# No GpSimd weight parts beside the first half of the gates' table, and every fourth expert tile there in plain float32

## Chip, cores and metric

One core of a Trainium2 chip runs the kernel. The metric is the device time of one execution in microseconds (us); smaller is better. TensorE (PE) multiplies, VectorE (DVE), ScalarE (ACT) and GpSimd (POOL) work on elements, SyncE (SP) issues most of the transfers.

## What is computed

A transformer layer, then two more. The first layer ends in a feed-forward part called PEER: each of its 256 tokens picks 128 of 16,384 single-neuron experts by product keys. The changed code lies in that part alone:

```python
q = (ht @ w_q).reshape(T, PEER_HEADS, PEER_QDIM)
s1 = einsum('thd,nd->thn', q[..., :PEER_HALF], sub_k1)
s2 = einsum('thd,nd->thn', q[..., PEER_HALF:], sub_k2)
...
gates = jax.nn.softmax(vals, axis=-1)
...
```

For the chosen experts, with input rows `expert_u` and output rows `expert_v`, the output is the sum over experts of gate times gelu(h · u) times v. Everything is float32.

## The kernel before

The kernel doesn't gather experts. It computes all 16,384 of them for all tokens and multiplies by a table of gates that is zero where an expert wasn't chosen. The experts come in 64 blocks of 256, and each block has two tiles (j = 0, 1) of 128 experts. `peer_block` (L983) does this in stages:

- **Heads** (L1044 to L1076): scores and top-16 lists. A queue of side work (`Side`) is stepped between them. It holds the keys' side products of later layers, and then `expert_in` of blocks 0 to 15 (`AHEAD`, L985).
- **Index work** (L1081 to L1145): VectorE turns the lists into the gates' coordinates. The side queue is stepped here too.
- **First half of the table**, `build_gates(0)` (L1203): 32 steps of 8 tokens. In each, VectorE makes one-hot tiles `o2` (L1169) and `o1` (L1171) and two scaled copies `og` (L1175), PE multiplies them in 16 small matmuls (L1178), and ACT copies the result into the table `G` (L1181). Between the steps the side queue advances by 21 tiles in all (`left`, L1202): tile 1 of block 5, and blocks 6 to 15.
- **Outgoing blocks 0 to 15** (L1207): `expert_out` scales the activations by the gates and multiplies them with `v` into four PSUM accumulators.
- **Blocks 16 to 63** (L1214): `expert_in(b + 1)`, with steps of `build_gates(1)` between while there are any, then `expert_out(b)`.

A float32 product is made in one of two ways. The **split** way (`wsplit`, `split_into`, `mm3`): ACT rounds the weights to `whi` (L295), another engine subtracts to get `wlo` (L296), and three matmuls in a reduced float32 format add up to full precision (L309 to L311), 24 for one expert tile with its eight slices of the model's width. The **plain** way (L1007): PE multiplies the raw weights `wraw` and the float32 activations `h2F`, eight matmuls for a tile, with no work on ACT or VectorE. `native[0]` chooses: it is False in the heads, True in the index work (set at L1079), and False again from L1148. Who subtracts is set by `K.pool_every`: with 2 (L1147) every second weight tile goes to GpSimd, with 0 all go to VectorE; L1206 sets 0 after the first half of the table.

Weights arrive by SP in transfers of 1 MB, a block's `u` or `v`, into three `wraw` buffers taken in turn. In blocks 16 to 63 the order is u(b+1), v(b), u(b+2), v(b+1), so the transfer of v(b+1) takes the buffer of u(b+1) and waits for its last reader. The split parts have three buffers each. Each engine runs its instructions in the order in which a planner put them.

`h2F` (8 KB in a partition) lies in the pool `p2f`, which closes with the index work. The pool `p2a` (16 activations of 2 KB) closes at L1209, and `p2h` (one table quarter of 32 KB) opens in its place.

Of the kernel before, what the change touches and what calls it, by code (L numbers as in the profile page):

```python
# [9 lines left out]
F32 = mybir.dt.float32  # L10
# [10 lines left out]
S = 256  # L21
NT = 2
KD = D // 128
# [941 lines left out]
def mem_values(K, pool2, mT, layer, tag):  # L965

    nc = K.nc
    for n in range(2):
        ps = [K.ps(tag) for _ in range(NT)]
        yield from K.gemm_tok_gen(ps, mT, f"xv{layer}", n * 4, 8)  # L970
        for t in range(NT):
            o = K.t(pool2, [128, 512], F32, tag="kvo")
            nc.scalar.activation(o, ps[t], AF.Copy)
            nc.sync.dma_start(K.kv[layer][:, t * D + n * 512:t * D + (n + 1) * 512], o)
# [8 lines left out]
def peer_block(K, x1, mT, close_mem):  # L983
# [5 lines left out]
    with ExitStack() as ctx:  # L989
        P = K.pool("p2", 1, ctx, side="right")  # L990
        P2 = K.pool("p2b", 2, ctx, side="right")
        ahead = ExitStack()
# [1 line left out]
        h2T = K.new_xT()  # L994
        GA = {}

        native = [False]

        def expert_in(b, tag="f"):
            ps = K.ps(tag)  # L1000
            pv = ps.rearrange("p (j n) -> p j n", j=2)
            raw = K.raw(("u", b), K.ins["u"][b].rearrange("p j k e -> p j (k e)"))
            for j in range(2):
                if native[0]:

                    for k in range(KD):
                        nc.tensor.matmul(pv[:, j], raw[:, j, k * 128:(k + 1) * 128], h2F[:, k, :],  # L1007
                                         start=k == 0, stop=k == KD - 1)
                else:
                    K.gemm_feat(pv[:, j], h2T, K.wsplit(raw[:, j], 8))  # L1010
                if j == 0:
                    yield
            GA[b] = K.t(GAP, [128, 2, S], F32, tag="ga") if b < AHEAD else K.t(P2, [128, 2, S], F32, tag="ga2")
            nc.scalar.activation(GA[b], pv, AF.Gelu_apprx_tanh)
            yield

        with ExitStack() as c2:
            F = K.pool("p2f", 1, c2)
            h2F = K.t(F, [128, KD, S], F32, tag="h2F")
            with ExitStack() as c3:  # L1020
                K.tmp = K.pool("tmp2", 2, c3)
                K.rms_T(K.tmp, x1, "norm2", h2T, h2F)
# [9 lines left out]
            def top16(src, val, idx, scr):  # L1032
# [5 lines left out]

            side = Side(mem_values(K, K.mt, mT, 0, "acc"), mem_values(K, K.mt, mT, 1, "acc"),
                        *[expert_in(b, "acc") for b in range(AHEAD)])  # L1040
            side.step(RS)
            K.pool_every = 1
# [33 lines left out]
                side.step(KVH)  # L1076
            pending.pop()()
            K.pool_every = 0
            native[0] = True  # L1079

            io16 = K.t(R, [128, 16], BF16, tag="io16")  # L1081
            nc.vector.tensor_copy(io16, K.cst("iota16"))
# [61 lines left out]
                nc.vector.tensor_copy(GP[:, 0, sl], GT[:, sl])  # L1144
                nc.vector.tensor_tensor(GP[:, 1, sl], GT[:, sl], GP[:, 0, sl], op=ALU.subtract)  # L1145

            K.pool_every = 2  # L1147
            native[0] = False  # L1148

        close_mem()  # L1150
        PG = K.pool("p2g", 2, ctx)
# [3 lines left out]
        def build_gates(half):  # L1155
            for q in (2 * half, 2 * half + 1):
                G[q] = K.t(PG2 if q == 2 else PG, [128, 32, S], F32, tag="G")
            b2, b1 = [128, 4, 128, 2], [128, 4, 64, 2]
            io2 = iota2[:, None].to_broadcast(b2)
            io1 = iota2[:, None, half * 64:half * 64 + 64].to_broadcast(b1)  # L1160

            def tokens(a, t0, shape):
                return a[:, t0:t0 + 8].rearrange("p (a b) -> p a b", a=4)[:, :, None, :].to_broadcast(shape)

            for t0 in range(0, S, 8):
                ps = K.ps()
                pv = ps.rearrange("p (t n) -> p t n", t=8)
                o2 = K.t(P2, b2, F16, tag="o2", bufs=GBUF)
                nc.vector.tensor_tensor(o2, io2, tokens(IT[1], t0, b2), op=ALU.is_equal)  # L1169
                o1 = K.t(P2, b1, F16, tag="o1", bufs=GBUF)  # L1170
                nc.vector.tensor_tensor(o1, io1, tokens(IT[0], t0, b1), op=ALU.is_equal)  # L1171
                og = []
                for j in range(2):
                    og.append(K.t(P2, b1, F16, tag=f"og{j}", bufs=GBUF))
                    nc.vector.tensor_tensor(og[j], o1, tokens(GP[:, j], t0, b1), op=ALU.mult)  # L1175
                for i in range(8):
                    for j in range(2):
                        nc.tensor.matmul(pv[:, i], o2[:, i // 2, :, i % 2], og[j][:, i // 2, :, i % 2],  # L1178
                                         start=j == 0, stop=j == 1, skip_group_check=True)
                for q in range(2):  # L1180
                    nc.scalar.activation(G[2 * half + q][:, :, t0:t0 + 8],  # L1181
                                         pv[:, :, q * 32:(q + 1) * 32].rearrange("p t n -> p n t"), AF.Copy)
                yield
# [27 lines left out]
        side = Side(build_gates(1))  # L1211
        for _ in expert_in(AHEAD):
            pass
        for b in range(AHEAD, 64):  # L1214
            if b < 63:
                for _ in expert_in(b + 1):
                    side.step(1)
            expert_out(b)
# [243 lines left out]
def layer_kernel(ctx: ExitStack, tc: tile.TileContext, ins, out):  # L1462
# [34 lines left out]
    K.mt = K.pool("mt", 2, held)  # L1497
    x1, mem = attention_block(K, x)
    x2 = peer_block(K, x1, mem, held.close)
    K.tmp = K.pool("tmp3", 2)  # L1500
    xT = K.new_xT()
# [29 lines left out]
```

## Time and profile before

| | us |
|---|---|
| median of 3 runs (1878.97 to 1880.27) | 1879.25 |
| the profiled execution | 1878.24 |
| its span in the trace | 1876.4 |
| PE busy | 1827.8 (97%) |
| VectorE busy | 1230.8 (66%) |
| ACT busy | 924.5 (49%) |
| GpSimd busy | 242.7 (13%) |

The span is from the first to the last instruction on the core; some 2 us around it belong to the execution's own time. Busy times of engines overlap. A matmul's duration holds its way through the array, so the time that it costs is read from the starts of matmuls that follow each other, not from the durations. An engine that is not the bound may idle at no cost.

### The profile page before, as it was taken

What the parts mean: (1) busy time and instruction counts of PE and PEld (TensorE: products, weight loads), DVE (VectorE), ACT (ScalarE), POOL (GpSimd) and SP (SyncE); (2) the same over time, 40 slices, a digit from 0 to 9 for tenths busy, and PEclk for the clock granted to TensorE, in tenths of its full rate; (3) what the DMA queues carried; (4) which work ended last, traced back from release to release, by engine and by line L of the source; (5) the groups of instructions that cost most, each with busy time, mean ns of one, the idle gap of its engine ahead of it and who ended that gap; (6) DMA issues with size and microseconds to landing.
All of it is one profiled execution on the core that took longest, in us unless ns stands there. A gap on an engine that the chain in (4) does not pass through costs nothing.

```text
span 1876.4 us, 31063 instructions
## 1 busy us (share of the span) xinstructions
PE 1827.8 (97%) x12627; PEld 1648.9 (88%) x12627; DVE 1230.8 (66%) x2094; ACT 924.5 (49%) x1527; POOL 242.7 (13%) x149
## 2 busy tenths in 40 slices
PE   7999999999999999999999999999999999989998
PEld 5798989889788989999999998988999899979997
DVE  5757657999866777555555557555566766646667
ACT  5554458445554555444444445443555545425453
POOL 2710237033000000000000000111100111120000
PEclk9999999999999999999999999999999999989999
DMA  7541445443454444555555557553556556525552
GB/s 268 180 158 46 136 171 191 161 177 114 159 197 173 168 164 174 177 183 180 188 193 181 182 191 284 180 178 114 177 183 201 183 180 204 199 90 202 173 190 110
DMA packets 78320, 326.39 MB, mean 174 GB/s; under 512 B 5856, under 2 KB 6496, under 8 KB 69600
## 3 DMA queue, kind: packets, MB, share of 16 engines
q1 hardware_dynamic: 74864, 315.35, 48.8%
q10 hardware_dynamic: 3312, 9.05, 1.4%
q8 instruction: 99, 1.62, 0.3%
q14 instruction: 45, 0.37, 0.1%
HBM read 321.23 MB, written 3.15 MB: 173 GB/s over the span
## 4 chain that ended last, share of the span: by engine, by line
PE 90%; DVE 6%; ACT 1%; DMA 1%; POOL 1%; issue 1%; ACTq 0%; POOLq 0%; SPq 0%; DVEq 0%
PE f L309 14%; PE f L311 14%; PE f L310 14%; PE acc L310 12%; PE acc L309 12%; PE acc L311 12%; PE acc L1007 2%; PE t L1178 1%; DVE og L1175 1%; PE acc L793 1%; DMA wraw<-in_stream 1%; PE f L1386 1%; PE acc L769 1%; DVE wlo L296 1%; PE t L395 1%
## 5 line engine op out<-in xcount | busy, mean ns | idle before, releaser
L295 ACT ACTIVATE whi<-wraw 128x1024 fp32r<-128x1024 f32 x528 | 557.3, 1057 | 575.9 <-PE f L310 311.5
L296 DVE TENSOR_TENSOR wlo<-wraw,whi 128x1024 fp32r<-128x1024 f32 x463 | 570.1, 1232 | 376.5 <-ACT whi L295 375.8
L309 PE MATMUL f<-xTh,whi 128*128 128x256 f32 x2016 | 574.1, 285 | 2.5 <-ACT xTh L295 2.5
L311 PE MATMUL f<-xTh,wlo 128*128 128x256 f32 x2016 | 573.6, 285 | 0.0
L310 PE MATMUL f<-xTl,whi 128*128 128x256 f32 x2016 | 572.5, 284 | 0.5 <-DVE xTl L296 0.5
L309 PEld LDWEIGHTS f<-xTh,whi 128*128 128x128 f32 x2016 | 386.5, 192 | 10.4 <-ACT xTh L295 3.4
L310 PEld LDWEIGHTS f<-xTl,whi 128*128 128x128 f32 x2016 | 387.0, 192 | 6.2 <-DVE xTl L296 1.2
L311 PEld LDWEIGHTS f<-xTh,wlo 128*128 128x128 f32 x2016 | 387.1, 192 | 2.5 <-issue 0.7
L296 POOL TENSOR_TENSOR wlo<-wraw,whi 128x1024 fp32r<-128x1024 f32 x65 | 160.0, 2470 | 556.3 <-ACT whi L295 390.3
L310 PE MATMUL acc<-wlo,wth 128*128 128x512 f32 x512 | 190.9, 396 | 0.0
L311 PE MATMUL acc<-whi,wtl 128*128 128x512 f32 x512 | 186.3, 395 | 1.1 <-DVE wtl L296 1.1
L309 PE MATMUL acc<-whi,wth 128*128 128x512 f32 x512 | 175.8, 397 | 0.9 <-ACT wth L295 0.9
L311 PEld LDWEIGHTS acc<-whi,wtl 128*128 128x128 f32 x512 | 96.0, 188 | 24.3 <-DVE wtl L296 1.5
L309 PEld LDWEIGHTS acc<-whi,wth 128*128 128x128 f32 x512 | 96.3, 188 | 22.5 <-ACT wth L295 1.0
L310 PEld LDWEIGHTS acc<-wlo,wth 128*128 128x128 f32 x512 | 96.2, 188 | 21.0
L295 ACT ACTIVATE wth<-gw 128x256 fp32r<-128x256 f32 x128 | 52.4, 411 | 83.7 <-PE acc L310 80.7
L1239 POOL MEMSET sgw<- 64x256 f32 x1 | 0.3, 307 | 671.6 <-DVE wlo L296 671.6
L1175 DVE TENSOR_TENSOR og<-o,gp 128x512 f16<-128x512 f16 x128 | 69.7, 554 | 23.3 <-PE t L1178 23.3
L296 DVE TENSOR_TENSOR wtl<-gw,wth 128x256 fp32r<-128x256 f32 x128 | 53.9, 423 | 34.3 <-ACT wth L295 19.2
L310 PE MATMUL acc<-wlo,xTh 128*128 128x512 f32 (+1 forms) x160 | 61.8, 388 | 2.5 <-POOL wlo L296 1.6
L311 PE MATMUL acc<-whi,xTl 128*128 128x512 f32 (+1 forms) x160 | 61.8, 386 | 0.0
L295 ACT ACTIVATE zhi<-wraw 128x1024 fp32r<-128x1024 f32 x44 | 44.7, 1052 | 31.5 <-PE acc L311 19.2
(324 smaller groups left out, 2852.8 us busy)
## 6 DMA issues: line engine op xcount, KB each, us to landing
wraw<-in_stream SPq DMA_DIRECT2D x162, 1024.0 KB, 5.0
wraw<-in_u SPq DMA_DIRECT2D x64, 1024.0 KB, 4.8
wraw<-in_v SPq DMA_DIRECT2D x64, 1024.0 KB, 4.9
lng<-in_rows ACTq DMA_DIRECT2D x6, 512.0 KB, 4.0
lnb<-in_rows ACTq DMA_DIRECT2D x6, 512.0 KB, 4.9
lnr<-in_mem SPq DMA_DIRECT2D x4, 512.0 KB, 6.9
kv<-kvo SPq DMA_DIRECT2D x8, 256.0 KB, 3.0
VR<-kv SPq DMA_DIRECT2D x2, 1024.0 KB, 5.6
```

The lines of the kernel that those rows point to most:

```text
L295: nc.scalar.activation(hi, src, AF.Copy)
L296: (lo_engine or nc.vector).tensor_tensor(lo, src, hi, op=ALU.subtract)
L309: mm(out, lhs[0], rhs[0], start=start, stop=False, **kw)
L310: mm(out, lhs[0], rhs[1], start=False, stop=False, **kw)
L311: return mm(out, lhs[1], rhs[0], start=False, stop=stop, **kw)
L395: nc.tensor.transpose(pv[:, j], src[:, (c + j) * 128:(c + j + 1) * 128], self.ident)
L769: nc.tensor.matmul(YT[t, br][s * 64:(s + 1) * 64, i * 128:(i + 1) * 128], lhs, rhs, start=first, stop=last, skip_group_check=True)
L793: nc.tensor.matmul(pv[:, j], QKT[s * 64:(s + 1) * 64, q0 + i, t * 128:(t + 1) * 128], QKT[s * 64:(s + 1) * 64, k_of(i), 0:nkey], start=Fal ...
L1007: nc.tensor.matmul(pv[:, j], raw[:, j, k * 128:(k + 1) * 128], h2F[:, k, :], start=k == 0, stop=k == KD - 1)
L1175: nc.vector.tensor_tensor(og[j], o1, tokens(GP[:, j], t0, b1), op=ALU.mult)
L1178: nc.tensor.matmul(pv[:, i], o2[:, i // 2, :, i % 2], og[j][:, i // 2, :, i % 2], start=j == 0, stop=j == 1, skip_group_check=True)
L1386: nc.tensor.matmul(pyv[:, dc], VR[:, mt, k * 128:(k + 1) * 128], pT[hp][:, hh * 2 + mt, :], start=mt == 0, stop=mt == NT - 1)
```

## The change

GpSimd no longer takes weight parts while the first half of the table is built: `K.pool_every` stays at the 0 that the index work set. `native` becomes a function of block and tile. In the heads it is always false, in the index work always true, and after that it is true for the second tile of every odd block. For the plain tiles `h2F` must live longer, so it moves to a pool on the right side that closes with `ahead` (L1209 of the kernel before).

```diff
-        native = [False]
+        native = [lambda b, j: False]
+        h2F = K.t(K.pool("p2f", 1, ahead, side="right"), [128, KD, S], F32, tag="h2F")
...
             for j in range(2):
-                if native[0]:
+                if native[0](b, j):
                     for k in range(KD):
                         nc.tensor.matmul(pv[:, j], raw[:, j, k * 128:(k + 1) * 128], h2F[:, k, :],
...
         with ExitStack() as c2:
-            F = K.pool("p2f", 1, c2)
-            h2F = K.t(F, [128, KD, S], F32, tag="h2F")
...
             K.pool_every = 0
-            native[0] = True
+            native[0] = lambda b, j: True
...
-            K.pool_every = 2
-            native[0] = False
+            native[0] = lambda b, j: b % 2 == 1 and j == 1
```

## Rows read from the trace of the kernel before

**Rows 1.** The page: busy time by engine, and the chain that ended last
```profile
PE 1827.8 (97%) x12627; PEld 1648.9 (88%) x12627; DVE 1230.8 (66%) x2094; ACT 924.5 (49%) x1527; POOL 242.7 (13%) x149
PE 90%; DVE 6%; ACT 1%; DMA 1%; POOL 1%; issue 1%; ACTq 0%; POOLq 0%; SPq 0%; DVEq 0%
```

**Rows 2.** Busy time by stretch: start:end, us, PE PEld DVE ACT POOL, PEclk, DMA
```profile
345.00:391.00 46.00, 46.00 (x219) 39.85 (x218) 43.38 (x117) 14.13 (x33) 6.11 (x2) 1.00 0.45 161
391.00:482.00 91.00, 84.31 (x1057) 80.43 (x1053) 88.81 (x149) 47.50 (x100) 24.27 (x9) 1.00 0.40 141
...
564.00:700.00 136.00, 136.00 (x1073) 122.20 (x1072) 97.23 (x148) 68.47 (x113) 0.00 (x0) 1.00 0.49 171
...
785.00:1130.00 345.00, 345.00 (x2182) 311.29 (x2181) 191.69 (x216) 164.20 (x216) 0.00 (x0) 1.00 0.55 188
```

**Rows 3.** One period of the first half of the table, same columns
```profile
433.88:442.18 8.30, 7.71 (x97) 7.41 (x97) 8.27 (x15) 4.36 (x9) 2.40 (x2) 1.00 0.36 126
```

**Rows 4.** Groups by form, from 395 to 482 us
```profile
L1175 DVE TENSOR_TENSOR og<-o,gp 128x512 f16<-128x512 f16 x64 | 43.0, 686 | 1.8 <-PE t L1178 1.8
...
L296 POOL TENSOR_TENSOR wlo<-wraw,whi 128x1024 fp32r<-128x1024 f32 x9 | 24.3, 2696 | 54.2 <-ACT whi L295 54.2
...
L296 DVE TENSOR_TENSOR wlo<-wraw,whi 128x1024 fp32r<-128x1024 f32 x12 | 14.6, 1218 | 0.0
```

**Rows 5.** Timeline of GpSimd, then VectorE, in that period
```profile
433.82 2.41 POOL L296 TENSOR_TENSOR wlo<-wraw,whi 128x1024 fp32r<-128x1024 f32 x1 [5.89 <-ACT whi L295]
...
433.87 2.63 DVE L1175 TENSOR_TENSOR og<-o,gp 128x512 f16<-128x512 f16 x1
...
437.03 0.41 DVE L1175 TENSOR_TENSOR og<-o,gp 128x512 f16<-128x512 f16 x1
```

**Rows 6.** Timeline of PE, 466 to 484 us: a table step's wait, the tail
```profile
466.40 0.66 PE L1178 MATMUL t<-og,o 128*128 128x64 f16 x16
466.90 0.36 PE L311 MATMUL acc<-xTh,wlo 128*128 128x256 f32 x1
...
470.37 0.94 PE L1178 MATMUL t<-og,o 128*128 128x64 f16 x16 [0.46 <-DVE o L1169]
...
479.58 0.50 PE L309 MATMUL acc<-whi,wth 128*128 128x512 f32 x1 [0.89 <-ACT wth L295]
...
482.81 1.20 PE L311 MATMUL acc<-whi,wtl 128*128 128x512 f32 x4 [1.10 <-DVE wtl L296]
```

**Rows 7.** Plain tiles: all instructions of L1007, then a stretch of the chain
```profile
L1007 PE MATMUL acc<-h2F,wraw x176: 377/379/382, 344.3 to 390.3; 128*128 128x256 f32 x176
...
377.30 13.38 PE acc L1007 x62
```

**Rows 8.** Timeline of PE, 391 to 394 us: split tile, back to back
```profile
391.77 0.28 PE L309 MATMUL acc<-xTh,whi 128*128 128x256 f32 x1
...
394.05 0.28 PE L310 MATMUL acc<-xTl,whi 128*128 128x256 f32 x1
```

**Rows 9.** The chain: first product group of two blocks, thirty blocks apart
```profile
785.82 0.94 PE acc L309 x4
...
1126.03 0.93 PE acc L309 x4
```

**Rows 10.** Timeline of SP and ACT in a block; landing times
```profile
912.95 0.38 SPq L322 DMA_DIRECT2D wraw<-in_v  x1
...
919.03 1.06 ACT L295 ACTIVATE whi<-wraw 128x1024 fp32r<-128x1024 f32 x1 [1.76 <-PE f L310]
...
924.84 1.05 ACT L295 ACTIVATE whi<-wraw 128x1024 fp32r<-128x1024 f32 x1
...
wraw<-in_v SPq DMA_DIRECT2D x64, 1024.0 KB, 4.9
...
band<-in_band ACTq DMA_DIRECT2D x1, 1024.0 KB, 11.3
```

## The prediction

> **What bounds the kernel now.** I read the page first: PE is busy for 97% of the span and makes up 90% of the chain that ended last; VectorE is 6% of that chain [rows 1]. So nearly everywhere a microsecond more on PE is a microsecond more of time, and elsewhere some stretch must wait for VectorE. The table of stretches shows which. From 391 to 482 us, while the first half of the gates' table is built, VectorE is busy 88.81 of 91 us and PE has 6.69 us without work. From 564 us on, where the incoming blocks 17 to 63 run, PE has no idle time at all: 136.00 of 136, 345.00 of 345 [rows 2].
>
> The groups and the timeline say why VectorE is full. An `og` copy takes 0.41 us, but their mean in this stretch is 0.686 [rows 4, 5]: in each period of 8.30 us [rows 3] one starts just after a weight part on GpSimd and lasts 2.63 us, as long as the GpSimd instruction does [rows 5]. While GpSimd subtracts, VectorE stands still. PE then waits for one-hot tiles (0.46 us in that period, and its 16 matmuls drag from 0.50 to 0.77 us) [rows 6].
>
> **The change part by part.** What decides is how far the new choice reaches. The function set after the index work is not replaced at the end of the first half. Blocks 17, 19, ..., 63 ask it as well, and it is true for their second tile. So six tiles become plain beside the first half of the table (second tiles of 5, 7, ..., 15), and 24 more in the PE-bound stretch behind it. That `h2F`'s pool has closed by then takes nothing away: `p2h` has the 32 KB of `p2a`, and `h2F` lies beside them.
>
> *Price of a plain tile on PE.* Its eight matmuls leave 16 records (176 for the eleven tiles of the index work), and 62 of them follow each other in 13.38 us [rows 7], 0.216 each: 16 x 0.216 = 3.45 us. A split tile's matmuls start 0.12 us apart (19 steps in 2.28 us) [rows 8]: 24 x 0.12 = 2.88. A plain tile costs PE 0.57 us more. The granted clock was 1.00 in the stretch with the plain tiles and is 1.00 later [rows 2], the 2.4 GHz level, so the prices can be carried over. It saves one ACT rounding and one subtraction.
>
> *A page on the same price.* The Trainium skill (FP8 and Floating Point Precision, section TensorE Precision Notes) counts four passes through the array for a true float32 product. At the 0.12 us of a split pass that makes 32 x 0.12 = 3.84 us for a tile, 0.96 more than a split one, against the 0.57 that the rows give.
>
> *First half of the table, the removed part.* In the 91 us PE needs 21 split tiles x 2.88 = 60.5 us, 31 steps x 16 matmuls at 0.50 [rows 6], and 0.08 at each return to the tiles (0.36 instead of 0.28) [rows 6, 8], which is 18.0, and some 2 us of the first outgoing block from 479.58 on [rows 6]. That is 80.5 us; 10.5 are lost, more than the profile's 6.69 idle, since a starved matmul drags on as a long one. VectorE would shed the stretched part of the 64 copies, 64 x (0.686 - 0.41) = 17.7 us. It takes the ten subtractions that GpSimd had, less the six that vanish: four x 1.22 [rows 4] = 4.9. So VectorE would need 88.8 - 17.7 + 4.9 = 76 us, less than PE's 80.5 + 6 x 0.57 = 83.9, and PE becomes the bound here. ACT, busy 47.50 of 91 us [rows 2], covers the rest, and loses six roundings. What stays lost is the tail: PE waits 0.89 and 1.10 us for the scaled activations of block 0 [rows 6], a chain through ACT and VectorE that no load of GpSimd makes. New length 83.9 + 2.0 = 85.9 us: a **gain of 5.1**. Bounds: all lost time comes back, 10.5 - 3.4 = 7.1 gained; nothing comes back, because the planned order still holds PE to VectorE's steps, 3.4 lost. I stay near the upper one, since the stretched copies, the row behind the waits, go altogether.
>
> *Second half, the added part.* 24 x 0.57 = **13.7 us more**, all of it on the path, since PE is busy without a gap there and a period is 11.34 us of matmuls (30 blocks in 340.21) [rows 9]. What ACT and VectorE save lies beside PE and is worth nothing. Bounds from the rows: 12 us, if a few switches to the other kind fall into pauses, and 15, if each block pays 0.08 for the switch.
>
> *Transfers.* In a block with a plain tile the buffer of `u` is free only when PE has done with it, not when the parts are split. SP now issues the `v` load at 912.95 and ACT reads it at 924.84 [rows 10]. Then it would be issued at PE's end of that block, about 919.03 [rows 10] + 0.57 = 919.6, and land 4.9 us later [rows 10], at 924.5; ACT wants it at 925.4. Behind it on SP stands the next `u` load, which slips by a microsecond and is wanted later still. I cost it at nothing: the cover is 0.9 us, and behind that the split runs ahead of PE. If PE reaches this `v` 11.34 us after 919.03, at 930.4, and the two parts take 2.3, the split can start at 928.1 instead of 924.84, so 3.3 us more.
>
> *The moved tile and lists.* `h2F` is written once, from the same normalised rows, and no wait is added: whoever lands on its old bytes waits already for the index work. Cost nothing, at most a microsecond either way from the new order.
>
> **The sum**, against the profiled execution's 1878.24: - 5.1 + 13.7 = + 8.6, 1886.8. The median of the runs is 1.0 above that execution, so **1887.8**.
>
> **The rivals.**
> - *Faster: the plain tiles end with the first half.* If the closed pool kept blocks from 17 on from the plain way, only the gain of 5.1 would stand: 1874.2. It decides at the choice that block 17 reads. For it: the words of the change. Against it: nothing sets the function back. 6%.
> - *VectorE's relief counts in full.* If the stretch were VectorE's alone, it would shrink to 76 us, a gain of 15, and with 13.7 given back the time is 1878: no change. Against it: PE's matmuls alone fill 83.9 us. 6%.
> - *Late weights.* If the `v` load, now close behind a `u` load, took the 11.3 us of the slowest 1 MB transfer [rows 10], it would land at 930.9, 2.2 after the last moment (928.1 + 0.57). PE then stalls in 24 blocks: 53 us, 1941. Against it: the 4.9 us median of 64 loads in this kernel. 4%.
> - *Four full passes.* A plain tile at 32 passes of 0.12 is 0.96 dearer than a split one: 24 x 0.96 = 23.0, and the first half gains 10.5 - 2.0 - 5.8 = 2.7 only. That is + 20.3, 1899.5. This is the page's count named above; the eleven plain tiles in the trace took 3.45 us, so it hardly holds. 3%.
>
> **How the numbers follow.** The forecast has 81%. Its own bounds are - 7.1 + 12 = + 4.9 (1884.2) and + 3.4 + 15 = + 18.4 (1897.7); the second needs the whole first half to fail. I give 1881 to 1895, a little below the lower bound because the engines' order is planned anew, and leave the rivals out, 19% together. A measurement of this kernel tells apart about 0.2%, 3.8 us. Slower by more than that: forecast but for a few per cent of it, late weights and four passes, 0.84. Within it: 0.09. Faster: 0.07.
>
> **What the profile after would show.** Right: no GpSimd weight part between 390 and 490 us, `og` copies all at 0.41, that stretch some 5 us shorter with PE as its bound; plain matmuls in 41 tiles, 656 records, two thirds of them past the first half, and a period of two blocks of 23.25 us in place of 22.68. Wrong: no plain record after the first half; a plain tile far from 3.45 us; PE waiting for ACT `whi` of a late `v` in odd blocks; or a first half that stays at 91 us.

## The result and the profile after

The changed kernel takes 1888.91 us (median of 6 runs, 1885.17 to 1891.70), against 1878.74 of the kernel before (6 runs): a ratio of 1.0058, 95% interval 1.0046 to 1.0069, or 10.2 us more. The forecast was 1887.8, slower, for two reasons that pull apart. Its profiled execution took 1888.58 us, with a span of 1886.8.

The page's busy times and its chain answer to [rows 1]:

```profile
PE 1842.7 (98%) x12387; PEld 1652.7 (88%) x12387; DVE 1190.1 (63%) x2075; ACT 896.6 (48%) x1497; POOL 213.1 (11%) x138
...
PE 93%; DVE 3%; DMA 1%; ACT 1%; POOL 1%; issue 0%; ACTq 0%; POOLq 0%; SPq 0%; DVEq 0%
```

PE is busier by 14.9 us, and VectorE's share of the chain has gone from 6% to 3%. The stretches, with the columns of [rows 2]:

```profile
345.00:391.00 46.00, 46.00 (x214) 39.80 (x214) 42.90 (x121) 13.67 (x35) 0.00 (x0) 1.00 0.45 160
391.00:482.00 91.00, 89.27 (x1026) 83.80 (x1025) 78.73 (x162) 44.74 (x98) 0.00 (x0) 1.00 0.42 143
...
564.00:700.00 136.00, 136.00 (x1019) 121.01 (x1018) 89.96 (x140) 62.26 (x105) 0.00 (x0) 1.00 0.49 167
...
785.00:1130.00 345.00, 345.00 (x2023) 306.64 (x2022) 170.37 (x193) 145.38 (x194) 0.00 (x0) 1.00 0.52 180
```

While the first half of the table is built, PE is now busy for 89.27 of 91 us (84.31 before) and VectorE for 78.73 (88.81 before). Behind it PE has no gap, as before. GpSimd has nothing to do in any of them. The groups by form from 391 to 482 us answer to [rows 4]:

```profile
L1174 DVE TENSOR_TENSOR og<-o,gp 128x512 f16<-128x512 f16 x68 | 27.1, 419 | 9.4 <-PE t L1177 9.3
...
L296 DVE TENSOR_TENSOR wlo<-wraw,whi 128x1024 fp32r<-128x1024 f32 x17 | 20.8, 1223 | 2.3 <-ACT whi L295 2.1
```

The mean of an `og` copy is 0.419 us, where it was 0.686, and the longest takes 0.427: no copy is stretched any more.

To see where the 10.4 us of the two spans lie, I take marks among the VectorE instructions that write the residual rows: the last addition of the attention part (L936), the first addition of the experts' sums (L1223 before, L1222 after), and the last layer norm's addition (L520). The lines give the first and the last start of each. Before, then after:

```profile
L520 DVE SCALAR_TENSOR_TENSOR lnr<-x,acc x24: 669/686/689, 1209.6 to 1868.2; 128x512 f32<-128x512 f32 x24
...
L936 DVE TENSOR_TENSOR x<-x,acc x4: 678/680/680, 239.8 to 251.2; 128x512 f32<-128x512 f32 x4
L1223 DVE TENSOR_TENSOR x<-x,acc x4: 680/680/681, 1134.0 to 1135.8; 128x512 f32<-128x512 f32 x4
```

```profile
L520 DVE SCALAR_TENSOR_TENSOR lnr<-x,acc x24: 670/686/690, 1218.9 to 1878.5; 128x512 f32<-128x512 f32 x24
...
L936 DVE TENSOR_TENSOR x<-x,acc x4: 680/680/681, 240.3 to 251.7; 128x512 f32<-128x512 f32 x4
L1222 DVE TENSOR_TENSOR x<-x,acc x4: 678/680/681, 1143.2 to 1145.0; 128x512 f32<-128x512 f32 x4
```

| | before | after | difference |
|---|---|---|---|
| to the end of attention | 251.2 | 251.7 | + 0.5 |
| to the first full group of the outgoing blocks, [rows 6] and below | 231.6 | 227.0 | - 4.6 |
| to the experts' sums | 651.2 | 664.5 | + 13.3 |
| to the end of the span | 742.4 | 743.6 | + 1.2 |

The mark between them, inside the block stage, is the first group of `wtl` products on PE, at 482.81 before [rows 6]. PE's timeline at the same place after:

```profile
474.58 0.95 PE L1177 MATMUL t<-og,o 128*128 128x64 f16 x16 [0.61 <-DVE o L1168]
...
476.30 0.51 PE L309 MATMUL acc<-whi,wth 128*128 128x512 f32 x1 [0.77 <-ACT wth L295]
...
478.67 1.20 PE L311 MATMUL acc<-whi,wtl 128*128 128x512 f32 x4 [0.23 <-DVE wtl L296]
```

It is at 478.67, and PE's waits around it (0.61, 0.77, 0.23) sum to 1.6 us. Forecast were - 5.1 for the first half and + 13.7 for the second.

The plain matmuls after, first those of the second half, then those up to block 15:

```profile
L1009 PE MATMUL f<-h2F,wraw x384: 377/379/459, 576.1 to 1132.1; 128*128 128x256 f32 x192
...
L1009 PE MATMUL acc<-h2F,wraw x272: 377/379/460, 344.8 to 472.6; 128*128 128x256 f32 x136
```

384 records are 24 tiles from 576 us on, and 272 are the 11 of the index work and six more. In the chain, two plain tiles of neighbouring odd blocks:

```profile
803.10 3.46 PE f L1009 x16
...
826.38 3.46 PE f L1009 x16
```

A plain tile holds PE for 3.46 us, and two blocks take 23.28, where two periods took 22.68 before [rows 9].

### The profile page after: what moved, and what is told of

Read it like the earlier page. It is cut to its first block, busy times and chain, and to the rows that moved or that the text cites. A ratio compares the mean times of both kernels' runs of the same rounds, so it can differ in the third digit from the quotient of the medians.

```text
span 1886.8 us, 30500 instructions
## 1 busy us (share of the span) xinstructions
PE 1842.7 (98%) x12387; PEld 1652.7 (88%) x12387; DVE 1190.1 (63%) x2075; ACT 896.6 (48%) x1497; POOL 213.1 (11%) x138
## 4 chain that ended last, share of the span: by engine, by line
PE 93%; DVE 3%; DMA 1%; ACT 1%; POOL 1%; issue 0%; ACTq 0%; POOLq 0%; SPq 0%; DVEq 0%
PE acc L311 13%; PE acc L310 13%; PE acc L309 13%; PE f L309 13%; PE f L311 13%; PE f L310 13%; PE f L1009 4%; PE acc L1009 3%; PE t L1177 2%; PE acc L793 1%; DMA wraw<-in_stream 1%; PE f L1385 1%; PE acc L769 1%; PE t L395 1%; PE t L819 0%; PE acc L1361 0%
## 5 line engine op out<-in xcount | busy, mean ns | idle before, releaser
L295 ACT ACTIVATE whi<-wraw 128x1024 fp32r<-128x1024 f32 x498 | 524.9, 1055 | 481.2 <-PE f L310 235.3
L309 PE MATMUL f<-xTh,whi 128*128 128x256 f32 x1824 | 519.0, 285 | 2.2 <-ACT xTh L295 2.2
L310 PE MATMUL f<-xTl,whi 128*128 128x256 f32 x1824 | 517.8, 284 | 0.5 <-DVE xTl L296 0.5
L311 PE MATMUL f<-xTh,wlo 128*128 128x256 f32 x1824 | 518.4, 284 | 0.0
L309 PEld LDWEIGHTS f<-xTh,whi 128*128 128x128 f32 x1824 | 348.4, 191 | 9.9 <-ACT xTh L295 3.1
L310 PEld LDWEIGHTS f<-xTl,whi 128*128 128x128 f32 x1824 | 348.9, 191 | 6.3 <-DVE xTl L296 1.2
L311 PEld LDWEIGHTS f<-xTh,wlo 128*128 128x128 f32 x1824 | 348.9, 191 | 2.5 <-issue 0.7
L296 POOL TENSOR_TENSOR wlo<-wraw,whi 128x1024 fp32r<-128x1024 f32 x54 | 129.7, 2411 | 449.9 <-ACT whi L295 446.2
L1009 PE MATMUL f<-h2F,wraw 128*128 128x256 f32 x384 | 87.4, 380 | 0.0
L1009 PEld LDWEIGHTS f<-h2F,wraw 128*128 128x128 f32 x384 | 71.2, 190 | 8.8
```

What stands on the lines that cost most here:

```text
L295: nc.scalar.activation(hi, src, AF.Copy)
L296: (lo_engine or nc.vector).tensor_tensor(lo, src, hi, op=ALU.subtract)
L309: mm(out, lhs[0], rhs[0], start=start, stop=False, **kw)
L310: mm(out, lhs[0], rhs[1], start=False, stop=False, **kw)
L311: return mm(out, lhs[1], rhs[0], start=False, stop=stop, **kw)
```

## The experiments

My theory: the first half gains because PE no longer waits for VectorE, the second half pays 0.57 us for each plain tile, and the two don't touch each other. Rivals: the first half pays too; the plain tiles' late release of weight buffers costs something; or the planner's new order does. For each run the table at the end of this section gives the *block stage* (from the last start of L936 to the first start of L1222 or L1223, as above) beside the median, because the code behind that stage, which no run changes, took between 732 and 743 us in the profiles. The stage is read from one profiled execution of each kernel; where a kernel was profiled twice, its two stages differ by 0.9 to 1.1 us. Diffs are against the changed kernel.

**The plain tiles end with block 15.**

```diff
-            native[0] = lambda b, j: b % 2 == 1 and j == 1
+            native[0] = lambda b, j: b < AHEAD and b % 2 == 1 and j == 1
```

> The plain tiles end with block 15; the rest is as in the changed kernel. My theory (the second half pays 24 x 0.57 us on a PE without gaps, the first half gains about 5): 1874 us, 4 to 5 under the kernel before, with the first product of the outgoing blocks as early as in the changed kernel and two blocks every 22.68 us from then on. Rival (the first half itself pays, and the later plain tiles are hidden or have little to do with it): within 3 us of the changed kernel, 1886 to 1892.

1873.65 us, ratio to the kernel before 0.9983 (0.9974 to 0.9992). The two marks of the block stage:

```profile
L936 DVE TENSOR_TENSOR x<-x,acc x4: 680/682/682, 238.5 to 250.0; 128x512 f32<-128x512 f32 x4
L1222 DVE TENSOR_TENSOR x<-x,acc x4: 681/682/683, 1128.1 to 1129.8; 128x512 f32<-128x512 f32 x4
```

The stage is 878.1 us long, 4.7 less than before, where 5.1 were forecast. The rival falls: with the later plain tiles gone, the change is a gain.

**Only the later tiles are plain; the first half is that of the kernel before.**

```diff
+            K.pool_every = 2
-            native[0] = lambda b, j: b % 2 == 1 and j == 1
+            native[0] = lambda b, j: b >= AHEAD and b % 2 == 1 and j == 1
```

> The first half of the table is as in the kernel before (GpSimd takes every second weight part, all tiles split); only the second tiles of blocks 17, 19, ..., 63 are plain. My theory: 13 to 14 us over the kernel before, 1892, and two blocks every 23.28 us once the table is done. Rival (the two parts hang together: the plain tiles' late release of weight buffers or another planned order takes part of the time): under 1888 or over 1896.

1893.53 us, ratio 1.0087 (1.0072 to 1.0101).

```profile
L936 DVE TENSOR_TENSOR x<-x,acc x4: 680/680/682, 239.9 to 251.4; 128x512 f32<-128x512 f32 x4
L1223 DVE TENSOR_TENSOR x<-x,acc x4: 680/682/683, 1147.5 to 1149.3; 128x512 f32<-128x512 f32 x4
```

The stage is 896.1 us, 13.3 more than before: 24 tiles at 0.55 us. PE's timeline at the first group of `wtl` products:

```profile
482.95 1.20 PE L311 MATMUL acc<-whi,wtl 128*128 128x512 f32 x4 [1.10 <-DVE wtl L296]
```

That is as far behind the end of attention as before (231.6 us), though `h2F` lies in its new pool and the order is planned anew: neither costs anything there. The two halves add up: - 4.7 + 13.3 = + 8.6, and the changed kernel's stage is 891.5 - 882.8 = 8.7 longer. The median is 15.9 over the kernel before, 2 more than my theory said; in the profile that excess lies behind the block stage (737.6 us against 734.2).

**No GpSimd part, and no plain tile after the index work.**

```diff
-            native[0] = lambda b, j: b % 2 == 1 and j == 1
+            native[0] = lambda b, j: False
```

> GpSimd takes no weight part beside the first half of the table, and no tile is plain after the index work. By the sums of the prediction PE needs 82.5 us in that stretch and VectorE 76 + 6 x 1.22 = 83.3: the two stand level, and the gain over the kernel before is 6 to 7, 1872, since six plain tiles no longer cost 3.4 us on PE. Rival (VectorE needs the relief of the plain tiles, or PE waits behind it all along): a gain under 3 us, 1876 or more, with PE waiting for one-hot tiles again.

1873.51 us, ratio 0.9981 (0.9972 to 0.9990); the stage gains 4.3 of the 6 to 7 expected. Neither side was right. PE shows no wait from 391 to 468 us. At the end of the table it waits for ACT and VectorE; PE's timeline:

```profile
470.08 0.64 PE L1177 MATMUL t<-og,o 128*128 128x64 f16 x16 [1.10 <-ACT G L1180]
...
472.36 0.61 PE L1177 MATMUL t<-og,o 128*128 128x64 f16 x15 [1.26 <-DVE og L1174]
...
473.75 0.73 PE L309 MATMUL acc<-whi,wth 128*128 128x512 f32 x1 [0.77 <-ACT wth L295]
```

The last table steps wait for the copies in `G` and for `og`, and the first outgoing product for its scaled activations: 1.10 + 1.26 + 0.77 = 3.1 us. Then comes something that I hadn't expected, in the stretches (columns as in [rows 2], the granted clock last but two):

```profile
474.00:477.00 3.00, 3.00 (x8) 2.36 (x8) 3.00 (x9) 0.00 (x1) 0.00 (x0) 0.50 0.00 0
```

After these pauses the granted clock is 0.50, that is 1.2 GHz, and PE's products of 128x512 start 0.43 us apart, where they start 0.23 apart from 478.20 us on.

**GpSimd takes every second part again; the six early tiles stay plain.**

```diff
+            K.pool_every = 2
-            native[0] = lambda b, j: b % 2 == 1 and j == 1
+            native[0] = lambda b, j: b < AHEAD and b % 2 == 1 and j == 1
```

> The six plain tiles beside the first half of the table stay, and GpSimd takes every second of the other weight parts again; none is plain later. My theory (the gain of the first half comes from the stretched copies, so with 7 GpSimd parts still there VectorE sheds 3 of 10 stretches and three subtractions, about 10 us, and PE, at 84 us, is near its bound already): 1875 to 1877. Rival (one stretched copy is enough to make PE wait in its period): no gain, 1878 to 1881.

1873.69 us, ratio 0.9981 (0.9971 to 0.9990); the stage gains 3.0. The groups by form from 391 to 482 us:

```profile
L1175 DVE TENSOR_TENSOR og<-o,gp 128x512 f16<-128x512 f16 x68 | 33.3, 510 | 13.0 <-PE t L1178 12.9
...
L296 POOL TENSOR_TENSOR wlo<-wraw,whi 128x1024 fp32r<-128x1024 f32 x7 | 19.8, 2824 | 50.6 <-ACT whi L295 41.9 <-DMA wraw<-in_u 8.7
```

Seven weight parts still run on GpSimd, but they stretch little: 68 copies at 0.510 us instead of 0.419 make 6.2 us, against the prediction's 17.7 for the kernel before. VectorE now waits 12.9 us for PE ahead of its copies, and parts of GpSimd's work fall into these waits. Only two copies last 2.4 us. One of them, and PE's table matmuls ahead of it and behind it:

```profile
415.16 1.11 PE L1178 MATMUL t<-og,o 128*128 128x64 f16 x31
415.80 2.41 DVE L1175 TENSOR_TENSOR og<-o,gp 128x512 f16<-128x512 f16 x1 [1.08 <-PE t L1178]
419.55 1.53 PE L1178 MATMUL t<-og,o 128*128 128x64 f16 x31
```

The 31 matmuls behind it take 1.53 us instead of 1.11, and 1.55 behind the other copy, so a full stretch still costs PE some 0.4 us. Behind the two copies of 1.26 us they take no longer than usual. The first outgoing product starts 225.2 us behind the end of attention, 0.7 later than in the run whose plain tiles end with block 15 (224.5). The other 1.0 of the 1.7 us between the two stages is the clock, which fell to 0.62 at the end of the table here too: from the first outgoing product to the next group of `wth` products PE takes 4.41 us, and 3.41 there. So in the first half each of the two edits does nearly the whole work without the other: without GpSimd 4.3, with plain tiles 3.0 (in both with the clock down at the end), both 4.7. That a stretched copy costs nothing isn't shown, since most of the stretch has gone.

**Only the last tile plain.** This and the next two ask where the six plain tiles are needed at all.

```diff
-            native[0] = lambda b, j: b % 2 == 1 and j == 1
+            native[0] = lambda b, j: b == 15 and j == 1
```

> No GpSimd part beside the first half of the table, and of its 21 tiles only the last one (second tile of block 15) is plain. My theory (with all tiles split, PE is the bound until the last three table steps; there VectorE is late, PE waits about 3 us and then runs at half the clock for some 4 us): a plain tile at the end costs PE 0.57 us and spares VectorE 1.2 just there, so half of that tail goes, 1871 to 1873. Rival (the tail is the chain from the last table step to the first outgoing block and does not care who is late): 1873.5 to 1875, with the half clock still there.

1870.75 us, ratio 0.9955 (0.9940 to 0.9970): faster than both kernels. The stage is 876.5, a gain of 6.3. PE's waits at the end of the table are short again (0.61, 0.33, 0.44 and 0.24; 1.6 in all, as in the changed kernel), with five plain tiles fewer ahead of them:

```profile
472.11 0.94 PE L1177 MATMUL t<-og,o 128*128 128x64 f16 x16 [0.61 <-DVE o L1168]
...
473.38 0.95 PE L1177 MATMUL t<-og,o 128*128 128x64 f16 x16 [0.33 <-DVE o L1168]
...
474.76 0.50 PE L309 MATMUL acc<-whi,wth 128*128 128x512 f32 x1 [0.44 <-ACT wth L295]
...
477.13 1.21 PE L311 MATMUL acc<-whi,wtl 128*128 128x512 f32 x4 [0.24 <-DVE wtl L296]
...
478.18 0.39 PE L309 MATMUL acc<-whi,wth 128*128 128x512 f32 x1
```

**The tiles of blocks 13 and 15, then both tiles of block 15.**

```diff
-            native[0] = lambda b, j: b % 2 == 1 and j == 1
+            native[0] = lambda b, j: b in (13, 15) and j == 1
```

```diff
-            native[0] = lambda b, j: b % 2 == 1 and j == 1
+            native[0] = lambda b, j: b == 15
```

> As the run with one plain tile, but the second tiles of blocks 13 and 15. My theory: PE needs 80.5 + 1.1, VectorE 76 + 4 x 1.22 = 80.9 and is ahead at the end; PE's waits of the tail shrink to 2 us and the clock stays up, so the stretch gains 6 to 7 over the kernel before, 1871 to 1872. Rival (tail unchanged): 1874 to 1875.

> As the run before, but both plain tiles at the very end: the two of block 15. My theory: the same sums, and VectorE free of weight parts for the last 7 us, so as fast as the run with the tiles of 13 and 15 or up to 1 us faster, 1870 to 1872. Rival (two plain tiles in a row hold the table's last matmuls back on PE, which the first outgoing block waits for): 1873 to 1875.

1875.59 us (0.9982, 0.9971 to 0.9993) and 1875.95 us (0.9983, 0.9973 to 0.9994), both later than either theory had. The stages, 877.7 and 876.8, are as expected; the loss against the run with one plain tile lies mostly behind the stage (736.9 us in both, 734.1 there).

**Every second tile of blocks 16 to 63 plain.**

```diff
-            native[0] = lambda b, j: b % 2 == 1 and j == 1
+            native[0] = lambda b, j: (b % 2 == 1 or b >= AHEAD) and j == 1
```

> The changed kernel, but from block 16 on the second tile of every block is plain, 48 in place of 24, so that every load of v waits for PE. My theory (a plain tile costs 0.57 us and nothing else): 13.7 us over the changed kernel, 1902 to 1903, and one block every 11.92 us. Rival (the load of v comes late once it waits for PE in each block, with the next u close behind it): PE waits for weights in most blocks, 1910 or more.

1898.95 us, ratio 1.0109 (1.0091 to 1.0126): 20.4 over the kernel before, so 10 over the changed kernel by the medians, less than the 13.7 expected. The stage, of one execution each, is 904.8 us, 13.3 more than in the changed kernel for 24 more tiles, 0.55 each as in the first 24. One block takes 11.94 us in the chain:

```profile
1056.74 3.45 PE f L1009 x16
1068.68 3.45 PE f L1009 x16
```

The loads by SP show why the weights are not late, though from 785 to 1130 us every `v` load waits for PE (the first line, of SP's waits in that stretch):

```profile
SPq L322 <- PE f L1009: 97.9, 29, 3.4
...
913.09 0.38 SPq L322 DMA_DIRECT2D wraw<-in_v  x1
916.94 0.33 SPq L322 DMA_DIRECT2D wraw<-in_u  x1
925.03 0.38 SPq L322 DMA_DIRECT2D wraw<-in_v  x1
```

The `v` load is issued 3.9 us before the next `u` load and 8.1 after the last one, so the transfers hardly overlap; the 64 `v` loads have a median of 5.0 us to landing. PE waits for nothing from 560 us to the end of the stage. The rival of late weights falls.

**Three of them again**, to tell the kernel's own share from the execution's: the kernels with one plain tile, with 13 and 15, and with block 15, unchanged.

> The same kernel as the run with one plain tile, a second time beside the two below. If its lead of some 5 us over the two runs with two plain tiles is the kernel's own (the stretch up to the outgoing blocks differs by 1 us only, the rest came behind the block stage), it is 1870 to 1872 again, with 734 us from the block stage's end to the last layer norm. If the rest belongs to the execution, it is within 2 us of the two others.

> The same kernel as the run with the plain tiles of blocks 13 and 15, a second time. Kernel's own: 1874 to 1877, 737 us behind the block stage, and half the clock at the tail again. The execution's: within 2 us of the run with one plain tile, the later stretch between 732 and 738, and the clock at the tail may stay full.

> The same kernel as the run with the two plain tiles of block 15, a second time. Kernel's own: 1874 to 1877, 737 us behind the block stage, full clock at the tail. The execution's: within 2 us of the run with one plain tile.

1871.57 us (0.9963, 0.9950 to 0.9976), 1875.42 (0.9985, 0.9976 to 0.9994) and 1875.79 (0.9986, 0.9976 to 0.9996). The medians are the kernels' own: each comes back within 1 us. The stretch behind the stage, expected at 737 us in the last two if it is the kernel's own, took 735.4 and 743.0 in their profiles, so one profile of it says little. The clock at the end of the table is not the kernel's own. With one plain tile, the first profile and the second, same columns as [rows 2]:

```profile
474.00:477.00 3.00, 2.46 (x19) 1.62 (x15) 3.00 (x8) 0.72 (x2) 0.00 (x0) 1.00 0.26 107
477.00:480.00 3.00, 2.87 (x12) 2.37 (x13) 3.00 (x10) 1.48 (x2) 0.00 (x0) 1.00 0.00 0
```

```profile
474.00:477.00 3.00, 2.56 (x20) 2.06 (x17) 3.00 (x7) 0.72 (x2) 0.00 (x0) 0.65 0.33 134
477.00:480.00 3.00, 3.00 (x11) 2.38 (x11) 3.00 (x9) 0.88 (x2) 0.00 (x0) 0.78 0.00 0
```

The same kernel had the full clock in the first and 0.65 and 0.78 of it in the second. Its pauses are the same; PE's timeline in the second:

```profile
472.22 0.94 PE L1177 MATMUL t<-og,o 128*128 128x64 f16 x16 [0.61 <-DVE o L1168]
473.49 0.94 PE L1177 MATMUL t<-og,o 128*128 128x64 f16 x16 [0.33 <-DVE o L1168]
474.88 0.79 PE L309 MATMUL acc<-whi,wth 128*128 128x512 f32 x1 [0.44 <-ACT wth L295]
...
479.34 0.39 PE L309 MATMUL acc<-whi,wth 128*128 128x512 f32 x1
```

From the first outgoing product to the next group of `wth` products PE takes 4.46 us here, and 3.42 at the full clock (474.76 to 478.18). With 13 and 15 it was the other way round, with block 15 the full clock came first. Where the clock fell, the stage was longer by 1.0, 0.9 and 1.1 us.

Behind the stage, the four profiles with two plain tiles have a wait that the two with one don't have. With 13 and 15, the first time, ACT, then PE:

```profile
1464.53 2.01 ACT L295 ACTIVATE zhi<-wraw 128x1024 fp32r<-128x1024 f32 x2 [1.32 <-DMA wraw<-in_stream]
1465.64 0.73 PE L309 MATMUL acc<-zhi,ysh 128*128 128x512 f32 x2 [0.83 <-ACT zhi L295]
```

ACT waits 1.26 to 1.39 us there for a transfer of later weights in the four, and PE 0.78 to 0.90 behind it; with plain tiles to block 15 the waits are 0.97 and 0.49. Why the transfer is late isn't shown.

| run | median | block stage | behind it, to L520 |
|---|---|---|---|
| before | 1878.74 | 882.8 | 734.2 |
| the change | 1888.91 | 891.5 | 735.3 |
| plain to block 15 | 1873.65 | 878.1 | 733.6 |
| plain from block 17 | 1893.53 | 896.1 | 737.6 |
| no GpSimd, all split | 1873.51 | 878.5 | 733.9 |
| GpSimd and early plain tiles | 1873.69 | 879.8 | 731.8 |
| last tile plain | 1870.75 | 876.5 | 734.1 |
| the same again | 1871.57 | 877.5 | 734.1 |
| 13 and 15 | 1875.59 | 877.7 | 736.9 |
| the same again | 1875.42 | 876.8 | 735.4 |
| block 15 | 1875.95 | 876.8 | 736.9 |
| the same again | 1875.79 | 877.9 | 743.0 |
| every second tile plain | 1898.95 | 904.8 | 738.4 |

## Why the prediction was right

- **The reach of the new choice** was read rightly: 24 plain tiles run after the first half, though the change's own words speak of the first half alone. This decides the sign.
- **The price of a plain tile**: 0.57 us was forecast, 0.55 was measured twice as a mean (13.3 us for 24 tiles, and 13.3 for 24 more). It isn't one price: where two blocks take 23.28 us instead of 22.68, a tile costs 0.60, so the earlier ones, most of them beside the second half of the table, cost less than 0.55; no run shows why. The second half came out at + 13.3 for + 13.7. The Trainium skill's count of four passes (FP8 and Floating Point Precision, TensorE Precision Notes) would have made it 23; the trace has 3.46 us for a tile, not 3.84, so the count with the split pass's price doesn't hold here.
- **The first half**: - 4.6 for - 5.1, with PE as the new bound, VectorE at 78.73 us where 76 were worked out, and 1.6 us of waits left at the tail where 2.0 were assumed. That the sum of both halves, + 8.7 in the stage, lies within 0.1 of the forecast + 8.6 is luck in part: one half missed by + 0.5, the other by - 0.4.
- **A reason that was too narrow.** I took the stretched copies for the thing whose removal makes the gain. Taking GpSimd out is one of two ways to it: with seven parts left on GpSimd and six tiles plain the stage still gained 3.0, but there most of the stretch went too (6.2 us left of 17.7). So it isn't shown whether PE needed the copies short or only VectorE less busy. By the prediction's count VectorE had 17.7 us of stretch to shed and PE only 10.5 - 2.0 = 8.5 to take, so part of the relief was worth nothing. The plain tiles beside the table were in part a second payment for the same thing: with five of the six split, the stage was 1.6 us shorter at the full clock (876.5 against 878.1).
- **A reading that was too wide.** VectorE doesn't stand still whenever GpSimd subtracts. In the kernel before, a GpSimd part that starts at 408.23 us lasts 4.85 instead of 2.4, while VectorE makes its next copies at 0.4 us each. The count of stretched copies, from their mean, isn't touched by this.
- **A share.** Of the 41 plain tiles 24, or 59%, lie past the first half, not two thirds.
- **Transfers** cost nothing, as forecast, and by a wider margin: the next `u` load comes 3.9 us behind the `v` load and not right on its heels.
- **The remainder**, 10.2 us by the medians for 8.6 in the sum: the stage accounts for 8.7, and the rest lies ahead of it and behind it (+ 0.5 and + 1.2 in the table of marks).

What stays open: why the code behind the block stage, which stands in the same order on every engine in the kernels with one and with two plain tiles at the end, is slower by 1.3 to 8.9 us in the profiles of the latter, and why the medians differ by 4 to 5 when the stages differ by at most 1.4. The repeats show that the difference of the medians belongs to the kernel, and the late transfer near 1464 us is some 0.9 us of it; no run shows the cause.

## What to carry to other kernels

Give a full engine's work away only as far as the next engine can use the room: here PE could take back some 8.5 us by the prediction's count, and one plain tile at the end of the stretch served better than six spread over it, by 0.6 and 1.6 us of the stage in two profiles (its median leads by more, but that part lies behind the stage and isn't explained). A switch that is set for one stage stays set for the next, so look for every later reader of it, and price it there too: the same tile that cost some 0.3 us beside a full VectorE (1.6 for five) costs its whole 0.55 us where PE has no gap.

## What I had not expected of the hardware

At the end of the table PE pauses for a few tenths of a microsecond several times in some 5 us (0.61, 0.33 and 0.44 with one plain tile). In one execution of that kernel the granted clock then fell to 0.65 and 0.78 over two stretches of 3 us, in another, with the same pauses, it stayed at 1.00. In the all-split run, with longer pauses, it was 0.50 from 474 to 477 us. The Trainium skill (TensorE: Matmul & The Clock Gate, Part 1) says that lack of activity takes the clock to half rate; the trace agrees on the level, but the pauses alone don't say whether it happens. In the three kernels that were profiled with both clocks, the stage was 0.9 to 1.1 us longer with the lower one.
